# A hybrid SSD and attention block: x projection's weights in pairs of feature tiles, eight token buffers, scaling on two engines in turn

## Chip, core and metric

The kernel runs on one core of one Trainium2 chip. The metric is the device time of one execution in microseconds (us); runs of the kernel before and of the changed one are compared by their medians.

## The reference, cut to what matters

```
def hybrid_layer(x, ...):                      # x: (1, 1024 tokens, 1024), float32
    h = rmsnorm(x, norm_mix_w)
    proj = h @ w_in                            # (1024 x 5664)
    z, xbc, dt_raw, q, k, v = jnp.split(proj, offs, axis=-1)
    y_ssm = ssd_mixer(z, xbc, dt_raw, ...)     # conv over time and SiLU on xbc, then chunked SSD
    y_na = neighbourhood_attention(q, k, v, ...)
    x = x + jnp.concatenate([y_ssm, y_na], axis=-1) @ w_out
    h = rmsnorm(x, norm_mlp_w)
    return x + jnp.square(jax.nn.relu(h @ w_mlp_in)) @ w_mlp_out
```

The change touches the beginning: the norm of x, its transpose, and the columns of `w_in` for `xbc` (1536 columns, twelve feature tiles of 128), called the x projection here.

## The kernel before, in words

Every product is made of three matmuls: each operand is split into hi (rounded, by ScalarE) and lo (the rest, by VectorE or GpSimd), and `mm3` adds hi·hi, hi·lo and lo·hi.

**Tokens.** The 1024 tokens are eight tiles t of 128 (x0 to x7 below). For each, SP loads `xt` (512 KB), an engine multiplies it by the norm's weights into `hn`, TensorE transposes `hn` in two halves of four (`ptn`, in PSUM), ScalarE writes the hi part `hTh` of each half and VectorE the lo part `hTl`. ScalarE also writes the squares' sum over `xt` in place (`sumsq`), three tiles later in the code, from which GpSimd makes the norm's factor `rcol`; TensorE spreads it over partitions (`dg` by VectorE, then the matmul `prr`, then `rrow` by ScalarE), and it scales the projection behind the matmuls. `xt` has six buffers, `hn` two; tiles 2 and 5 are multiplied on GpSimd, the others on VectorE. The two halves of a tile take their PSUM buffers from two tags of two buffers each, so a half waits until `hTh` and `hTl` of the same half two tiles before are written; `pp`, the transpose of a few parameters (`prow`), takes its buffer from the second tag, behind the second half of tile 7.

**Weights.** `load_w` loads 1024 columns' worth into a raw buffer (three of them), ScalarE writes hi, `lo_eng` lo (four slots). For the x projection `load_w_col` takes one feature tile, all 1024 rows by 128 columns, 512 bytes a row. Two tiles are loaded early, among the tokens (`early`, at t of 3 and 5). Feature tiles 8 to 11 come first (the SSD's B and C), in two pairs, with GpSimd for lo; then dt (`decays`), then tiles 0 to 7 one at a time, with VectorE for lo.

**Order.** `xbc` computes, for each token half h and each of its feature tiles, 24 matmuls (`proj_col`: eight k of `mm3`) into a PSUM buffer `px`, scales it into `ub`, and convolves `ub` over time (`conv`). A list scheduler places the instructions of all engines, each engine's queue being strictly in the order it fixed. SP's queue holds all loads, in order; behind the beginning's loads it has eight small transfers of the position biases (`t1_dr`, `t_dr` in the profile), which a later stage needs. Behind the x projection come z, the SSD, attention, the output projection and the MLP, which the change does not touch.

Of the kernel before, what the change touches and what calls it, by code (L numbers as in the profile page):

```python
# [9 lines left out]
F32 = mybir.dt.float32  # L10
# [3 lines left out]
AF = mybir.ActivationFunctionType  # L14
# [4 lines left out]
P = 128  # L19
T = 1024  # L20
D = 1024
NT = T // P
KD = D // P
PROJ = 5664
OFF_Z, OFF_X, OFF_DT, OFF_Q, OFF_K, OFF_V = 0, 1024, 2560, 2592, 3616, 4640
# [30 lines left out]
def hymba_block(  # L56
# [25 lines left out]
    nc = tc.nc  # L82
# [48 lines left out]
    half = cp.tile([P, 8], F32, name="half")  # L131
    nc.gpsimd.memset(half, -0.5)

    def load_w(view, lo_eng, n=1024):
        pool = phase["w"][phase["n"] % len(phase["w"])]
        nb = phase["w"].count(pool)
        phase["n"] += 1
        rpool = phase["r"][phase["n"] % len(phase["r"])]
        raw = rpool.tile(
            [P, 1024], F32, tag="wraw", name="wraw", bufs=phase["r"].count(rpool)  # L140
        )
        hi = pool.tile([P, 1024], F32R, tag="wh", name="wh", bufs=nb)
        lo = pool.tile([P, 1024], F32R, tag="wl", name="wl", bufs=nb)
        dst = raw[:, 0:n]
        if len(view.shape) == 3:
            dst = dst.rearrange("p (a f) -> p a f", a=view.shape[1])
        nc.sync.dma_start(dst, view)
        nc.scalar.activation(hi[:, 0:n], raw[:, 0:n], AF.Copy)  # L148
        lo_eng.tensor_tensor(  # L149
            lo[:, 0:n], raw[:, 0:n], hi[:, 0:n].bitcast(F32), op=sub  # L150
        )
        return hi, lo
# [11 lines left out]

        return get

    def load_w_col(src, c0, n, lo_eng):
        v = src[:, c0 : c0 + n]
        hi, lo = load_w(v.rearrange("(k p) f -> p k f", p=P), lo_eng, KD * n)

        def get(k):
            s = slice(k * n, (k + 1) * n)
            return hi[:, s], lo[:, s]

        return get

    def mm3(pt, ah, al, bh, bl, first, last):
        nc.tensor.matmul(pt, lhsT=ah, rhs=bh, start=first, stop=False)  # L178
# [2 lines left out]

    def split_from_psum(hi, lo, src, scalar=None):
        if scalar is None:
            nc.scalar.activation(hi, src, AF.Copy)  # L184
            nc.vector.tensor_tensor(lo, src, hi.bitcast(F32), op=sub)
        else:
            nc.scalar.activation(hi, src, AF.Copy, scale=scalar)
            nc.vector.scalar_tensor_tensor(
                lo, src, scalar, hi.bitcast(F32), op0=mul, op1=sub
            )  # L190
# [14 lines left out]
    def transpose_split(th, tl, t, hn):  # L205
        for g in range(2):
            pt = (ps_tp if g else ps_s)("ptn")
            for j in range(4):
                k = 4 * g + j
                nc.tensor.transpose(  # L210
                    pt[:, j * P : (j + 1) * P], hn[:, k * P : (k + 1) * P], ident
                )
            dst = (slice(None), slice(4 * g, 4 * g + 4), slice(t * P, (t + 1) * P))
            split_from_psum(th[dst], tl[dst], pt.rearrange("p (j t) -> p j t", j=4))

# [1 line left out]
    with ExitStack() as ph:  # L219
        enter_phase(ph, 1, 3, 1)  # L220
        hp = ph.enter_context(tc.tile_pool(name="hp", bufs=1))
        hTh = hp.tile([P, KD, T], F32R, name="hTh")
        hTl = hp.tile([P, KD, T], F32R, name="hTl")
# [14 lines left out]
        with ExitStack() as p0:  # L238
            xp = p0.enter_context(tc.tile_pool(name="xp", bufs=2, side="right", reuse_waits="tile"))
            wb = xp.tile([P, D], F32, name="wb", bufs=1)  # L240
            ssq = xp.tile([P, NT], F32, name="ssq", bufs=1)
            xb = x[0].rearrange("(i b j) d -> i b j d", b=8, j=8)
            xts = []
            early = {}

            def sumsq(t):
                nc.scalar.activation(
                    xts[t], xts[t], AF.Square, accum_out=ssq[:, t : t + 1]
                )

            for t in range(NT):
                xt = xp.tile([P, D], F32, tag="xt", name="xt", bufs=6)
                xts.append(xt)
                hn = xp.tile([P, D], F32, tag="hn", name="hn", bufs=2)
                eng = nc.gpsimd if t in (2, 5) else nc.vector
                for h in range(2):
                    s = slice(h * 512, (h + 1) * 512)
                    if t == 0:
                        nc.sync.dma_start(
                            wb[:, s], norm_mix_w.partition_broadcast(P)[:, 0, s]  # L260
                        )
                        nc.sync.dma_start(xt[:, s], xb[:, t, :, s])
                        if h == 0:
                            nc.sync.dma_start(ident, cst_d[:, 0:P])
                        eng.tensor_tensor(hn[:, s], xt[:, s], wb[:, s], op=mul)
                if t > 0:
                    nc.sync.dma_start(xt, xb[:, t])
                    eng.tensor_tensor(hn, xt, wb, op=mul)
                transpose_split(hTh, hTl, t, hn)
                if t >= 3:  # L270
                    sumsq(t - 3)
                if t in (3, 5):
                    ft = 8 + (3, 5).index(t)
                    early[ft] = load_w_col(w_in[0], OFF_X + ft * P, P, nc.gpsimd)
            for t in range(NT - 3, NT):
                sumsq(t)
            for h in range(2):
                s = slice(4 * h, 4 * h + 4)
                nc.gpsimd.tensor_scalar(rcol[:, s], ssq[:, s], 1.0 / D, EPS, op0=mul, op1=add)
                nc.gpsimd.tensor_tensor(rcol[:, s], rcol[:, s], half[:, s], op=ALU.pow)  # L280
# [30 lines left out]
        with ExitStack() as p1:  # L311
# [114 lines left out]

            def xbc(fts):
                todo = []
                for ft in fts:
                    eng = nc.gpsimd if ft > 7 else nc.vector  # L430
                    get = early.get(ft) or load_w_col(w_in[0], OFF_X + ft * P, P, eng)
                    ub = qp.tile([P, T + 4], F32, tag="ub", name="ub")
                    nc.gpsimd.memset(ub[:, 0:2], 0.0)
                    nc.gpsimd.memset(ub[:, T + 2 : T + 4], 0.0)
                    todo.append((ft, get, ub))
                for h in range(2):
                    for ft, get, ub in todo:
                        pt = ps_mm("px")
                        proj_col(get, P, h, pt)
                        nc.vector.tensor_tensor(  # L440
                            to_grid(ub[:, 2 : T + 2], h),
                            from_blocks(pt),
                            from_blocks(rrow[:, h * 512 : (h + 1) * 512]),
                            op=mul,
                        )
                for ft, get, ub in todo:
                    conv(ft, ub)
# [43 lines left out]
            xbc((8, 9))  # L491
            xbc((10, 11))
            decays()
            for ft in range(8):
                xbc((ft,))


            szb = sz_dr.rearrange("c p f -> (c p) f").rearrange(
# [2 lines left out]
            for g in range(2):  # L501
                get = load_w_nat(w_in[0], 0, KD, OFF_Z + 512 * g, nc.vector)
                for t in range(NT):
                    pt = ps_mm("pz")
# [268 lines left out]
    with ExitStack() as ph:  # L773
# [63 lines left out]
        done = [0]  # L837
# [539 lines left out]
```

## Time and profile before

| | |
|---|---|
| time, median of 3 runs | 1728.23 us (1726.64 to 1728.27) |
| the profiled execution | 1725.33 us, its span 1723.5 us |
| TensorE busy | 1636.0 us, 95% of the span |
| VectorE, ScalarE, GpSimd busy | 1106.3, 726.5, 705.6 us (64, 42, 41%) |
| TensorE's granted clock, mean of the span | 0.98 of full |

The span is what the trace covers of the execution; 1.83 us lie around it. Times in the rows count from the span's start. In a timeline's row the first number is the start, the second the length, and in brackets stands how long the engine was idle before it and what ended that. PE is TensorE's matmul, PEld its weight load, DVE VectorE, ACT ScalarE, POOL GpSimd, SP or SPq the queue that issues the loads. A matmul of 512 columns is listed with 0.39 us, but the next starts 0.23 us behind it, since they overlap; the pitch is what counts.

### The profile page before, as it was taken

The numbers are of one execution on the slowest core, as the hardware profiler recorded it, in microseconds if no ns is written. First come the engines' busy times: TensorE is split into PE (matmuls) and PEld (weight loads), VectorE is DVE, ScalarE is ACT, GpSimd is POOL, SyncE is SP. The second block draws the span as 40 slices with busy tenths as digits, with TensorE's granted clock in tenths as the row PEclk, the third lists the DMA queues.
The fourth block names the chain that finished last, engine by engine and source line by source line (L and its number), as shares of the span: only waits on it lengthen the run. The fifth ranks groups of instructions, "written<-read, shape, count | busy, mean of one in ns | idle before, by whom it ended". The sixth has DMA issues, their size and how long they took to land. (4 is left out here: it accounts for less than half of the span.)

```text
span 1723.5 us, 20879 instructions
## 1 busy us (share of the span) xinstructions
PE 1636.0 (95%) x7461; PEld 1304.6 (76%) x7461; DVE 1106.3 (64%) x1687; ACT 726.5 (42%) x1189; POOL 705.6 (41%) x496
## 2 busy tenths in 40 slices
PE   6999999989888999999999988999999978999999
PEld 5788888777766777777767767788888866888887
DVE  5767214889787744778787776454343359787863
ACT  5434223434344434555565533454444443333330
POOL 4000004888778741221242242244444426555551
PEclk9999999999998999999999999999999989999999
DMA  8213338876675796754453141254344394644231
GB/s 200 62 37 104 89 98 242 210 195 207 213 206 161 234 311 199 240 150 138 132 183 123 56 159 49 73 190 153 134 159 147 125 349 149 201 141 166 92 110 73
DMA packets 178499, 269.75 MB, mean 157 GB/s; under 512 B 13963, under 2 KB 105051, under 8 KB 178395
## 3 DMA queue, kind: packets, MB, share of 16 engines
q1 hardware_dynamic: 135419, 231.18, 42.6%
q10 hardware_dynamic: 42976, 37.23, 7.1%
q8 instruction: 59, 0.97, 0.2%
q14 instruction: 45, 0.37, 0.1%
HBM read 185.21 MB, written 86.50 MB: 158 GB/s over the span
## 5 line engine op out<-in xcount | busy, mean ns | idle before, releaser
L760 POOL TENSOR_TENSOR wl<-wraw,wh 128x1024 fp32r<-128x1024 f32 x110 | 300.1, 2740 | 350.1 <-ACT wh L759 336.7
L745 PE MATMUL px<-wh,ahl 128*128 128x512 f32 x512 | 163.7, 397 | 9.8 <-ACT ahl L759 9.8
L759 ACT ACTIVATE wh<-wraw 128x1024 fp32r<-128x1024 f32 x110 | 115.7, 1054 | 127.4 <-issue 42.4
L179 PE MATMUL pq<-wl,hTh 128*128 128x512 f32 x384 | 153.1, 400 | 4.6 <-DVE wl L149 4.4
L745 PE MATMUL px<-h,wh 128*128 128x512 f32 x496 | 156.5, 396 | 0.0
L178 PE MATMUL pq<-wh,hTh 128*128 128x512 f32 x384 | 153.1, 401 | 1.9 <-ACT wh L148 1.2
L180 PE MATMUL pq<-wh,hTl 128*128 128x512 f32 x384 | 151.9, 396 | 0.0
L759 ACT ACTIVATE ahl<-ar 128x1024 fp32r<-128x1024 f32 x56 | 58.9, 1053 | 173.0 <-PE px L745 89.6
L760 DVE TENSOR_TENSOR ahl<-ar,ahl 128x1024 fp32r<-128x1024 f32 x56 | 107.3, 1917 | 37.4 <-ACT ahl L759 36.2
L745 PEld LDWEIGHTS px<-wh,ahl 128*128 128x128 f32 x512 | 97.3, 190 | 31.9 <-ACT ahl L759 10.2
L745 PEld LDWEIGHTS px<-h,wh 128*128 128x128 f32 x496 | 93.4, 189 | 22.4
L149 DVE TENSOR_TENSOR wl<-wraw,wh 128x1024 fp32r<-128x1024 f32 x40 | 55.0, 1376 | 83.3 <-ACT wh L148 82.7
L878 POOL TENSOR_TENSOR mb<-braw,nam 128x256 f32<-128x256 f32 (+1 forms) x48 | 41.0, 884 | 159.7 <-DVE nmx L936 123.4
L184 ACT ACTIVATE pth<-ptp 128x384 fp32r<-128x384 f32 (+1 forms) x128 | 58.4, 459 | 107.8 <-PE ptp L959 106.8
L745 PE MATMUL px<-wl,ahl 128*128 128x512 f32 x256 | 100.9, 394 | 0.0
L745 PE MATMUL px<-h,wl 128*128 128x512 f32 x248 | 98.1, 396 | 0.0
L179 PEld LDWEIGHTS pq<-wl,hTh 128*128 128x128 f32 x384 | 73.2, 191 | 22.1 <-DVE wl L149 7.9
L149 POOL TENSOR_TENSOR wl<-wraw,wh 128x1024 fp32r<-128x1024 f32 x18 | 43.8, 2446 | 110.5 <-ACT wh L148 84.3
L745 PE MATMUL pz<-wh,ahl 128*128 128x512 f32 x256 | 82.8, 400 | 6.5 <-DVE acc L1330 5.0
L178 PEld LDWEIGHTS pq<-wh,hTh 128*128 128x128 f32 x384 | 72.9, 190 | 18.2 <-ACT wh L148 2.5
L180 PEld LDWEIGHTS pq<-wh,hTl 128*128 128x128 f32 x384 | 73.2, 191 | 14.7
L612 POOL TENSOR_TENSOR rb<-rb,c 128x512 f32<-128x512 f32 x64 | 75.0, 1192 | 21.5 <-DMA rb<-cum_dr 18.7
(265 smaller groups left out, 4242.6 us busy)
## 6 DMA issues: line engine op xcount, KB each, us to landing
act_dr<-cq SPq DMA_DIRECT2D x56, 512.0 KB, 3.0
ar<-act_dr SPq DMA_DIRECT2D x56, 512.0 KB, 3.8
wraw<-in_w_in_dram SPq DMA_DIRECT2D x44, 512.0 KB, 4.0
rb<-cum_dr SPq DMA_DIRECT2D x32, 512.0 KB, 7.6
wraw<-in_w_mlp_in_dram SPq DMA_DIRECT2D x32, 512.0 KB, 4.7
wraw<-in_w_mlp_out_dram SPq DMA_DIRECT2D x32, 512.0 KB, 5.3
q_dr<-hl ACTq DMA_DIRECT2D x64, 128.0 KB, 3.2
k_dr<-hl ACTq DMA_DIRECT2D x16, 512.0 KB, 3.2
```

Of the source, the lines that this page charges most:

```text
L149: lo_eng.tensor_tensor(lo[:, 0:n], raw[:, 0:n], hi[:, 0:n].bitcast(F32), op=sub)
L178: nc.tensor.matmul(pt, lhsT=ah, rhs=bh, start=first, stop=False)
L179: nc.tensor.matmul(pt, lhsT=ah, rhs=bl, start=False, stop=False)
L180: return nc.tensor.matmul(pt, lhsT=al, rhs=bh, start=False, stop=last)
L184: nc.scalar.activation(hi, src, AF.Copy)
L612: nc.gpsimd.tensor_tensor(rb[:, d], rb[:, d], c1[:, d, c, h0 : h0 + 4].unsqueeze(2).broadcast_to([P, 4, P]), op=sub,)
L745: nc.tensor.matmul(pt, lhsT=a, rhs=b, start=f, stop=l, skip_group_check=True)
L759: nc.scalar.activation(hl[0], src, AF.Copy)
L760: eng.tensor_tensor(hl[1], src, hl[0].bitcast(F32), op=sub)
L878: nc.gpsimd.tensor_tensor(mb[:, s].rearrange("p (s r c) -> p s r c", r=16, c=8), v[:, a:b], nam[:, s].rearrange("p (s r c) -> p s r c", r= ...
```

## The change

The x projection's weights are loaded for two feature tiles at once: `load_w_pair` makes two tiles of 512 rows by 256 columns (1 KB a row), each with the columns of both features, and gives a getter for either feature. The first pair (8, 9) is loaded at t = 3, the second (10, 11) at t = 5; the two tiles of the first are called W0 and W1 below, those of the second W2 and W3 (in the kernel before, these are the tiles of features 8 to 11). All twelve feature tiles now run in pairs. For the early pairs, hi is placed behind the last hi part of the token tile just transposed (`issue_after`, which sets the order only). `xt` has eight buffers, and the odd token tiles are multiplied on GpSimd, the even ones on VectorE.

```
--- before.py
+++ after.py
@@ -131,7 +131,7 @@
     half = cp.tile([P, 8], F32, name="half")
     nc.gpsimd.memset(half, -0.5)
 
-    def load_w(view, lo_eng, n=1024):
+    def load_w(view, lo_eng, n=1024, after=None):
         pool = phase["w"][phase["n"] % len(phase["w"])]
         nb = phase["w"].count(pool)
         phase["n"] += 1
@@ -145,7 +145,8 @@
         if len(view.shape) == 3:
             dst = dst.rearrange("p (a f) -> p a f", a=view.shape[1])
         nc.sync.dma_start(dst, view)
-        nc.scalar.activation(hi[:, 0:n], raw[:, 0:n], AF.Copy)
+        with tc.issue_after(after.ins) if after else ExitStack():
+            nc.scalar.activation(hi[:, 0:n], raw[:, 0:n], AF.Copy)
         lo_eng.tensor_tensor(
             lo[:, 0:n], raw[:, 0:n], hi[:, 0:n].bitcast(F32), op=sub
         )
@@ -164,15 +165,21 @@
 
         return get
 
-    def load_w_col(src, c0, n, lo_eng):
-        v = src[:, c0 : c0 + n]
-        hi, lo = load_w(v.rearrange("(k p) f -> p k f", p=P), lo_eng, KD * n)
-
-        def get(k):
-            s = slice(k * n, (k + 1) * n)
-            return hi[:, s], lo[:, s]
-
-        return get
+    def load_w_pair(src, c0, lo_eng, after=None):
+        tiles = []
+        for kh in range(2):
+            v = src[512 * kh : 512 * (kh + 1), c0 : c0 + 2 * P]
+            tiles.append(load_w(v.rearrange("(k p) f -> p k f", p=P), lo_eng, after=after))
+
+        def half(j):
+            def get(k):
+                hi, lo = tiles[k // 4]
+                s = slice((k % 4) * 2 * P + j * P, (k % 4) * 2 * P + j * P + P)
+                return hi[:, s], lo[:, s]
+
+            return get
+
+        return half(0), half(1)
 
     def mm3(pt, ah, al, bh, bl, first, last):
         nc.tensor.matmul(pt, lhsT=ah, rhs=bh, start=first, stop=False)
@@ -181,8 +188,9 @@
 
     def split_from_psum(hi, lo, src, scalar=None):
         if scalar is None:
-            nc.scalar.activation(hi, src, AF.Copy)
+            done = nc.scalar.activation(hi, src, AF.Copy)
             nc.vector.tensor_tensor(lo, src, hi.bitcast(F32), op=sub)
+            return done
         else:
             nc.scalar.activation(hi, src, AF.Copy, scale=scalar)
             nc.vector.scalar_tensor_tensor(
@@ -211,7 +219,8 @@
                     pt[:, j * P : (j + 1) * P], hn[:, k * P : (k + 1) * P], ident
                 )
             dst = (slice(None), slice(4 * g, 4 * g + 4), slice(t * P, (t + 1) * P))
-            split_from_psum(th[dst], tl[dst], pt.rearrange("p (j t) -> p j t", j=4))
+            done = split_from_psum(th[dst], tl[dst], pt.rearrange("p (j t) -> p j t", j=4))
+        return done
 
 
 
@@ -249,10 +258,10 @@
                 )
 
             for t in range(NT):
-                xt = xp.tile([P, D], F32, tag="xt", name="xt", bufs=6)
+                xt = xp.tile([P, D], F32, tag="xt", name="xt", bufs=8)
                 xts.append(xt)
                 hn = xp.tile([P, D], F32, tag="hn", name="hn", bufs=2)
-                eng = nc.gpsimd if t in (2, 5) else nc.vector
+                eng = nc.gpsimd if t % 2 else nc.vector
                 for h in range(2):
                     s = slice(h * 512, (h + 1) * 512)
                     if t == 0:
@@ -266,12 +275,12 @@
                 if t > 0:
                     nc.sync.dma_start(xt, xb[:, t])
                     eng.tensor_tensor(hn, xt, wb, op=mul)
-                transpose_split(hTh, hTl, t, hn)
+                turned = transpose_split(hTh, hTl, t, hn)
+                if t in (3, 5):
+                    ft = 8 + (t - 3)
+                    early[ft] = load_w_pair(w_in[0], OFF_X + ft * P, nc.gpsimd, turned)
                 if t >= 3:
                     sumsq(t - 3)
-                if t in (3, 5):
-                    ft = 8 + (3, 5).index(t)
-                    early[ft] = load_w_col(w_in[0], OFF_X + ft * P, P, nc.gpsimd)
             for t in range(NT - 3, NT):
                 sumsq(t)
             for h in range(2):
@@ -426,9 +435,10 @@
 
             def xbc(fts):
                 todo = []
-                for ft in fts:
-                    eng = nc.gpsimd if ft > 7 else nc.vector
-                    get = early.get(ft) or load_w_col(w_in[0], OFF_X + ft * P, P, eng)
+                ft = fts[0]
+                eng = nc.gpsimd if ft > 7 else nc.vector
+                gets = early.get(ft) or load_w_pair(w_in[0], OFF_X + ft * P, eng)
+                for ft, get in zip(fts, gets):
                     ub = qp.tile([P, T + 4], F32, tag="ub", name="ub")
                     nc.gpsimd.memset(ub[:, 0:2], 0.0)
                     nc.gpsimd.memset(ub[:, T + 2 : T + 4], 0.0)
@@ -491,8 +501,8 @@
             xbc((8, 9))
             xbc((10, 11))
             decays()
-            for ft in range(8):
-                xbc((ft,))
+            for ft in range(0, 8, 2):
+                xbc((ft, ft + 1))
 
 
             szb = sz_dr.rearrange("c p f -> (c p) f").rearrange(
```

The scheduler's order moves with it. On SP W0 and W1 now stand in front of x4 and W2 in front of x6; before, the tile of feature 8 stood in front of x4 and that of feature 9 in front of x6. On TensorE four matmuls of the projection now stand in front of tile 5's transposes and those of the first half of tile 6; before, 24 stood in front of tile 5's.

In SP's queue, behind the token loads, these rows stand before (wraw_469 and 478 are the tiles of features 10 and 11):

```order
L298 DMA cst_297<-cst_dram 128x384
L301 DMA lmask_299<-lmask_dram 128x128
L303 DMA dsk_301<-in_d_skip_dram 128x16
L147 DMA wraw_469<-in_w_in_dram 128x8x128
L147 DMA wraw_478<-in_w_in_dram 128x8x128
L527 DMA t1_dr_76<-in_rel_pos_bias_dram 16x15x24 x8
L147 DMA wraw_714<-in_w_in_dram 128x8x128
```

and now (wraw_243 is W3):

```order
L307 DMA cst_309<-cst_dram 128x384
L310 DMA lmask_311<-lmask_dram 128x128
L312 DMA dsk_313<-in_d_skip_dram 128x16
L537 DMA t1_dr_76<-in_rel_pos_bias_dram 16x15x24 x8
L147 DMA wraw_243<-in_w_in_dram 128x4x256
L147 DMA wraw_714<-in_w_in_dram 128x4x256
```

W3 has moved behind the eight transfers of the position biases; its raw buffer is the one that held W0.

On ScalarE, at the end of the token stage, these rows stand before (ptn_217 and 224 are the halves of tile 5, 242 and 249 of tile 6, 261 and 268 of tile 7; wh_470 and 479 are hi of features 10 and 11):

```order
L247 ACTIVATE xt_238,ssq_109<-xt_238 128x1024
L148 ACTIVATE wh_470<-wraw_469 128x1024
L184 ACTIVATE hTh_89<-ptn_217 128x4x128
L148 ACTIVATE wh_479<-wraw_478 128x1024
L184 ACTIVATE hTh_89<-ptn_224 128x4x128
L184 ACTIVATE hTh_89<-ptn_242 128x4x128
L247 ACTIVATE xt_257,ssq_109<-xt_257 128x1024
L184 ACTIVATE hTh_89<-ptn_249 128x4x128
L184 ACTIVATE hTh_89<-ptn_261 128x4x128
L184 ACTIVATE hTh_89<-ptn_268 128x4x128
```

and now (ptn_223 and 230 are the halves of tile 5, 254 and 261 of tile 6, 273 and 280 of tile 7; wh_238 and 244 are hi of W2 and W3):

```order
L191 ACTIVATE hTh_89<-ptn_223 128x4x128
L256 ACTIVATE xt_250,ssq_109<-xt_250 128x1024
L191 ACTIVATE hTh_89<-ptn_230 128x4x128
L149 ACTIVATE wh_238<-wraw_237 128x1024
L191 ACTIVATE hTh_89<-ptn_254 128x4x128
L149 ACTIVATE wh_244<-wraw_243 128x1024
L256 ACTIVATE xt_269,ssq_109<-xt_269 128x1024
L191 ACTIVATE hTh_89<-ptn_261 128x4x128
L191 ACTIVATE hTh_89<-ptn_273 128x4x128
L191 ACTIVATE hTh_89<-ptn_280 128x4x128
```

Hi of W3 stands in front of hTh of the second half of tile 6 and of both halves of tile 7.

On GpSimd, through the token stage, these rows stand before (hn_152 and 214 are tiles 2 and 5):

```order
L268 TENSOR_TENSOR hn_152<-xt_151,wb_108 128x1024
L149 TENSOR_TENSOR wl_190<-wraw_188,wh_189 128x1024
L279 TENSOR_SCALAR rcol_104<-ssq_109 128x4
L268 TENSOR_TENSOR hn_214<-xt_213,wb_108 128x1024
L280 TENSOR_TENSOR rcol_104<-rcol_104,half_78 128x4
L149 TENSOR_TENSOR wl_234<-wraw_232,wh_233 128x1024
L149 TENSOR_TENSOR wl_471<-wraw_469,wh_470 128x1024
L149 TENSOR_TENSOR wl_480<-wraw_478,wh_479 128x1024
```

and now (hn_134, 170, 220, 270 are tiles 1, 3, 5, 7; wl_189 and 195 are lo of W0 and W1):

```order
L277 TENSOR_TENSOR hn_134<-xt_133,wb_108 128x1024
L277 TENSOR_TENSOR hn_170<-xt_169,wb_108 128x1024
L288 TENSOR_SCALAR rcol_104<-ssq_109 128x4
L289 TENSOR_TENSOR rcol_104<-rcol_104,half_78 128x4
L277 TENSOR_TENSOR hn_220<-xt_219,wb_108 128x1024
L150 TENSOR_TENSOR wl_189<-wraw_187,wh_188 128x1024
L150 TENSOR_TENSOR wl_195<-wraw_193,wh_194 128x1024
L277 TENSOR_TENSOR hn_270<-xt_269,wb_108 128x1024
L150 TENSOR_TENSOR wl_239<-wraw_237,wh_238 128x1024
L150 TENSOR_TENSOR wl_245<-wraw_243,wh_244 128x1024
```

Lo of W0 has moved from before tile 5's multiplication to behind it.

## Rows read from the trace of the kernel before

**Rows 1.** Busy time by stretches of 5 us: engines, granted clock, DMA share, GB/s

```profile
15.00:20.00 5.00, 3.67 (x16) 3.27 (x16) 1.91 (x3) 2.66 (x5) 0.97 (x2) 1.00 1.06 232
20.00:25.00 5.00, 0.98 (x5) 1.01 (x6) 4.44 (x5) 3.90 (x8) 4.84 (x3) 0.83 1.10 245
25.00:30.00 5.00, 5.00 (x15) 3.97 (x15) 3.56 (x3) 3.12 (x5) 4.12 (x3) 0.50 0.37 100
```

**Rows 2.** Waits of TensorE, 30 to 285 us, whole answer: total, times, longest

```profile
PE px L178 <- ACT hTh L184: 0.2, 1, 0.2
```

**Rows 3.** Timeline 0 to 30 us: what started as loads landed, and SP

```profile
15.76 1.23 DVE L268 TENSOR_TENSOR hn<-xt,wb 128x1024 f32<-128x1024 f32 x1 [0.67 <-DMA xt<-in_x_dram]
...
18.71 1.06 ACT L148 ACTIVATE wh<-wraw 128x1024 fp32r<-128x1024 f32 x1 [1.72 <-DMA wraw<-in_w_in_dram]
...
20.56 2.71 DVE L268 TENSOR_TENSOR hn<-xt,wb 128x1024 f32<-128x1024 f32 x1 [2.98 <-DMA xt<-in_x_dram]
...
22.73 0.22 SPq L288 DMA_DIRECT2D prow<-in_k_norm_w_dram  x1
...
25.68 0.22 SPq L287 DMA_DIRECT2D prow<-in_q_norm_w_dram  x1
...
27.00 0.22 SPq L288 DMA_DIRECT2D prow<-in_k_norm_w_dram  x1
...
27.27 0.37 SPq L298 DMA_DIRECT2D cst<-cst_dram  x1
...
28.35 0.33 SPq L303 DMA_DIRECT2D dsk<-in_d_skip_dram  x1
28.72 1.06 SPq L147 DMA_DIRECT2D wraw<-in_w_in_dram  x2
```

**Rows 4.** The same timeline: GpSimd, VectorE and TensorE

```profile
19.84 2.35 POOL L149 TENSOR_TENSOR wl<-wraw,wh 128x1024 fp32r<-128x1024 f32 x1 [4.03 <-ACT wh L148]
...
24.02 1.09 PE L210 MATMUL ptn<-ident,hn 128*128 128x128 f32 x4 [4.48 <-DVE hTl L185]
...
26.82 2.38 POOL L149 TENSOR_TENSOR wl<-wraw,wh 128x1024 fp32r<-128x1024 f32 x1
...
27.11 3.17 DVE L268 TENSOR_TENSOR hn<-xt,wb 128x1024 f32<-128x1024 f32 x1 [1.44 <-DMA xt<-in_x_dram]
...
27.46 0.63 PE L179 MATMUL px<-hTl,wh 128*128 128x512 f32 x1
...
27.89 0.63 PE L180 MATMUL px<-hTh,wl 128*128 128x512 f32 x1
```

**Rows 5.** Timeline 30 to 60 us

```profile
29.82 7.32 SPq L527 DMA_DIRECT2D t_dr<-in_rel_pos_bias_dram  x8
...
33.24 1.03 PE L210 MATMUL ptn<-ident,hn 128*128 128x128 f32 x8
33.32 1.06 ACT L148 ACTIVATE wh<-wraw 128x1024 fp32r<-128x1024 f32 x1 [1.81 <-DMA wraw<-in_w_in_dram]
...
37.09 1.06 ACT L247 ACTIVATE xt<-xt 128x1024 f32<-128x1024 f32 x1
...
38.13 0.60 ACT L184 ACTIVATE hTh<-ptn 128x512 fp32r<-128x512 f32 x1
...
38.76 0.69 DVE L185 TENSOR_TENSOR hTl<-ptn,hTh 128x512 fp32r<-128x512 f32 x1 [0.72 <-ACT hTh L184]
...
40.02 0.39 PE L179 MATMUL px<-hTl,wh 128*128 128x512 f32 x1
...
40.24 0.39 PE L180 MATMUL px<-hTh,wl 128*128 128x512 f32 x1
...
42.55 0.80 PE L179 MATMUL px<-hTl,wh 128*128 128x512 f32 x1
```

**Rows 6.** Timeline of SP, 32.0 to 32.6 us

```profile
31.59 1.26 SPq L527 DMA_DIRECT2D t_dr<-in_rel_pos_bias_dram  x2
```

**Rows 7.** Waits of SP's queue, 0 to 60 us: total, times, longest

```profile
SPq L267 <- ACT hTh L184: 3.7, 1, 3.7
```

## Prediction, made before the changed kernel was run

> **What bounds the kernel now.** I read the page's totals first, then busy time by stretches, then the waits of TensorE, and last the first 48 us instruction by instruction. The totals (the table above) make TensorE by far the busiest engine. The stretches say where the missing part is: from 15 to 25 us TensorE has a few microseconds of work while the DMA engines are full, and from 25 us on it is always busy [rows 1]. From 30 to 285 us, which takes in the whole x projection, it waited 0.2 us in all [rows 2]. So the x projection is bound by TensorE; what another engine saves there is worth nothing, and the change can act only through the moment at which TensorE gets its work in the first 48 us. Everything later follows as a block.
>
> What bounds that beginning are the loads. Between the landing of x3 (VectorE starts on it at 15.76) and that of x7 (SP, which waited for it, goes on at 28.35) lie six transfers of 512 KB: W0, x4, x5, W1, x6, x7 at 18.71, 20.56, 22.73, 25.68, 27.00, 28.35 [rows 3]. That is 2.1 us each, with full DMA engines until 25 us [rows 1].
>
> **The change, part by part.**
>
> *Same work.* A pair of tiles holds the same 1024 x 256 weights as two column tiles did: as many bytes, hi and lo operations, matmuls and transposes. That is 0. In the middle of the projection each pair now needs both its tiles to its end, so a slot comes free later; the next pair's tiles are already in the other two slots, and a pair is 96 matmuls of 0.227 us, 21.8 us, far above the 1.06 + 1.23 us of a split (the ScalarE row at 33.32 in [rows 5], and 1.23 for 1024 columns on VectorE at 15.76 in [rows 3]). I count 0 here, and a us or two if one splits late.
>
> *Eight token buffers.* x6 and x7 no longer wait for ScalarE to have finished with x0 and x1. The DMA engines are full anyway [rows 1], so this alone moves no landing: 0.
>
> *More weights ahead of the tokens.* The first pair puts W0 and W1 before x4, the second pair's first tile W2 before x6. In slots after x3, with the times of before for slots 3 and 6: x4 is third (22.7), x5 fourth (24.7, between 15.76 + 4 x 2.1 = 24.2 and the 25.7 of W1's slot), x6 sixth (28.4), x7 seventh (28.4 + 2.1 = 30.5). So x5 lands 2.0 later than now, x6 1.4 and x7 2.1.
>
> *GpSimd scales the odd tokens.* One costs 2.35 there (as the 1024-column operation at 19.84 in [rows 4]) against 1.23 on VectorE [rows 3]. More important is what happens when the two engines meet. VectorE's scaling at 20.56 took 2.71 and the one at 27.11 took 3.17; in both cases a GpSimd operation was running (19.84 + 2.35 = 22.19, 26.82 + 2.38 = 29.20), and VectorE's end is 1.08 behind the end of that operation [rows 3, 4]. So an SBUF-only operation of one waits out that of the other. The Trainium skill, GPSIMD Engine Reference, section Key points, says that GpSimd shares its SBUF interfaces with VectorE instructions of two SBUF inputs, which speaks against alternating them. By that rule, which gives no price, the sum would only be some unknown amount above 0; the trace agrees and gives the price, waiting to the end.
>
> *Chain A, over GpSimd.* x5 lands 24.7; scaling on GpSimd until 27.05; GpSimd's lo of W0, now behind it in order, 2.38, until 29.45; VectorE's scaling of x6 (landed 28.4) waits for that, until 30.7; VectorE's lo of the first half of token tile 4 stands behind it (0.69), until 31.4. Only then is the PSUM buffer free for the first half of tile 6, and TensorE's queue holds it ahead of all but four matmuls of the projection. Before, 24 of them were done when tile 5 began at 33.24 [rows 5]. From 31.4: half a tile (0.5), 41 matmuls at 0.227 (40.02 to 40.24 in [rows 5]), 12 transposes at 0.129 (1.03 for 8 at 33.24) = 0.5 + 9.3 + 1.55, so TensorE stands at the transpose of the parameters (pp) at 42.75. With what follows (pp 0.2, three matmuls 0.7, one 0.23, prr 0.43) the second matmul of the second token half would come at 44.3. It began at 42.55 before [rows 5]. Chain A alone costs 1.75.
>
> *Chain B, over SP and ScalarE.* The second pair's second tile, W3, needs a raw buffer that GpSimd frees at 29.45, and SP has it behind the eight t1_dr transfers, where W2 and W3 stood in front of them. x7 lands 30.5; cst, lmask and dsk take 1.2 (27.27 to 28.72, less some 0.2 of waiting, [rows 3]); eight t1_dr issues (t_dr in the profile) go at 0.65 each where nothing blocks them (31.59 to 31.59 + 1.26 is two, [rows 6]), 5.2; so W3 is issued at 36.9 and lands 4.6 later, as W2 did (28.72 to ScalarE's start at 33.32, [rows 3, 5]): 41.5. In ScalarE's order W3's hi stands in front of the squares of tile 7, of hTh of tile 6's second half and of both halves of tile 7. So: hi 1.06, squares 1.06, hTh 0.60, lo on VectorE 0.69 [rows 5], and the PSUM buffer that pp needs is free at 44.9, 2.2 after TensorE came for it. On the second token half: hTh of tile 7 at 44.8, then VectorE's dg, which waits out GpSimd's lo of W3 (42.6 + 2.4 = 45.0) and takes 0.69, then lo 0.69: 46.4. TensorE's second matmul there starts at 46.6 instead of 42.55: **+4.05 us**. Behind it I find nothing that it could overtake: from 48 us on the queues hold the same work, and TensorE has no waits to give up [rows 2].
>
> The profiled execution took 1725.33, 2.9 below the median of the runs shown, 1728.23; by its own time the sum is 1729.4, and set on the median 1728.23 + 4.05 = **1732.3**.
>
> *Bounds.* Low: if W2 cost the loads nothing (x7 at 28.35 as now), chain B ends 2.1 earlier and chain A's +1.75 decides. High: t1_dr issues at their old average (7.32 for eight, [rows 5]) add 2.1: +6.15. I take 0.65 because the two slow ones stood behind W2 and W3 in flight, and none flies now. The clock: TensorE worked at half pace (0.43 a matmul at 27.46 to 27.89, [rows 4]) from 24.02 until 30, the end of the stretch with granted 0.50 [rows 1]. Now it works from about 23.9 to 29.6 and then waits 1.8. If the rise comes only after that wait, up to 6 us more run at half pace, 3.0 lost on chain A, of which chain B hides 2.2: +4.85.
>
> **Rivals.** The threshold of all chances is 0.2%, 3.5 us: about what a measurement of this kernel can tell from no change.
>
> 1. *Chain B decides* (forecast): 1732.3, own range +2.5 to +6.2. For it: ScalarE's order and SP's order are fixed, and 5.2 + 4.6 us lie between x7 and W3. Against: the 2.2 us margin over chain A hangs on a few waits. 50%, of which about 10 in 50 end under 3.5.
>
> 2. *Chain A decides alone*, W3 in time: +1.75, 1730.0. It needs W3 at 39.3 or earlier. A W's landing came 2.95 behind its predecessor, an x's 1.85 and 2.17 [rows 3]; if the larger pieces (1 KB, not 512 B) took away these 0.9 us three times, x7 would land at 27.8 and W3 at 38.8. The Trainium skill, DMA: Bandwidth & Descriptors, section Specifications, asks 512 B or more for line rate: by that rule the larger pieces gain nothing and the sum stays at +4.05, and the rows, where an x is sometimes as late, do not settle it. With 0.9 us less for each W the sum falls to chain A's, itself 1 us or so earlier, near +0.5. 30%.
>
> 3. *The clock falls in the new wait* before pp (2.2 us and the waits of 1 us behind it): the 4.48 us of idling before 24.02 [rows 4] went with a granted clock that fell to 0.83, then 0.50 [rows 1], the lower of its two levels (1.2 of 2.4 GHz). It would cost up to 6 us at half pace, 3.0: +7, 1735.3. Against: the wait is half as long. 10%.
>
> 4. *Faster:* the loads of x6 and x7 were held by their issue. SP waited 3.7 us for ScalarE with x6 [rows 7]; if issued at once, x6 and x7 landed so much earlier, the squares, rrow and the second token half would follow, and TensorE's idle 4.48 us and the half pace shrink: 1728.23 - 3.7 = 1724.5. It decides if x7 lands before 24.6. Against: full DMA engines from 15 to 25 [rows 1], and one W more in front. 7%; 3% are left for no change at all.
>
> **How the numbers follow.** Slower by over 0.2%: 40 of rival 1's 50, rival 3's 10 and 5 of rival 2 with late tiles: 0.55. Faster: 0.07. Within 0.2%: the rest, 0.38. The range 1728.0 to 1736.5 reaches from rival 2's low end to rival 3's and leaves out the faster case and the worst sums.
>
> **What the profile after would show.** If right: the DMA waits put x7 at 30 or later; ScalarE waits for the DMA of W3 around 41 with hTh behind it; TensorE waits for lo of VectorE at pp for about 2 us; VectorE's scaling of x6 takes over 1.23 if it starts before GpSimd's lo ends; four matmuls of the projection, then tile 5 and a gap near 30; and from 48 us on the same rows come 4 us later. Wrong would be: no wait at pp (chain B falls), matmuls back to back from 27 us (chain A falls), or a second half-pace stretch behind 43 us (rival 3).

## The result, and the profile after

The changed kernel took 1732.06 us, the median of 12 runs (1722.24 to 1735.29), against 1726.31 for the kernel before in 12 runs (1720.39 to 1728.89): ratio 1.0030, 95% interval 1.0017 to 1.0043. That is slower, with an interval clear of 1; the ratio is above the 0.2% that a measurement of this kernel can tell from no change, though the interval's lower end is not. Two further sets of runs gave 1.0039 (1.0025 to 1.0052) and 1.0027 (1.0015 to 1.0040).

The execution that was profiled happens to be the shortest of its twelve (span 1720.4 us), so two later profiles of the same kernel, with spans of 1734.2 and 1726.7, stand beside it below. The stretches of the first, which answer to [rows 1] (engines, granted clock, DMA share, GB/s):

```profile
15.00:20.00 5.00, 2.70 (x12) 1.90 (x10) 3.55 (x6) 4.49 (x8) 2.74 (x3) 1.00 1.06 268
20.00:25.00 5.00, 4.43 (x20) 3.74 (x20) 1.67 (x3) 4.71 (x9) 4.20 (x2) 1.00 1.04 279
25.00:30.00 5.00, 2.68 (x9) 2.33 (x10) 4.26 (x6) 3.07 (x5) 5.00 (x3) 0.68 0.34 71
```

The DMA engines are as full as before but move 268 and 279 GB/s instead of 232 and 245, and TensorE's busy time goes the other way round: 4.43 us from 20 to 25, where it had 0.98, and then a hole from 25 to 30, where it had none. TensorE's waits from 30 to 285 us are again a single row, as in [rows 2], now at `pp`:

```profile
PE pp L299 <- DVE hTl L192: 0.8, 1, 0.8
```

The hole is chain A of the prediction. The timeline (start, length, engine) with what answers to [rows 3, 4]:

```profile
20.80 2.36 POOL L277 TENSOR_TENSOR hn<-xt,wb 128x1024 f32<-128x1024 f32 x1 [1.70 <-DMA xt<-in_x_dram]
...
23.12 5.68 POOL L150 TENSOR_TENSOR wl<-wraw,wh 128x1024 fp32r<-128x1024 f32 x2
...
24.47 2.10 DVE L277 TENSOR_TENSOR hn<-xt,wb 128x1024 f32<-128x1024 f32 x1 [3.33 <-DMA xt<-in_x_dram]
...
26.49 2.47 DVE L192 TENSOR_TENSOR hTl<-ptn,hTh 128x512 fp32r<-128x512 f32 x4
...
27.32 1.08 PE L218 MATMUL ptn<-ident,hn 128*128 128x128 f32 x4 [2.80 <-DVE hTl L192]
...
29.05 0.63 PE L186 MATMUL px<-hTl,wh 128*128 128x512 f32 x1
29.48 0.63 PE L187 MATMUL px<-hTh,wl 128*128 128x512 f32 x1
```

x5 is scaled on GpSimd, lo of W0 follows in its queue, VectorE's scaling of x6 (2.10 instead of 1.23) waits that out, lo of tile 4 stands behind it, and TensorE idles 2.80 us for the PSUM buffer. Behind it the granted clock is 0.68 in the stretch from 25 to 30, and the matmuls follow each other at 0.43 us until 30. Chain B comes after it, in the rows that answer to [rows 5, 6]:

```profile
26.16 0.36 SPq L307 DMA_DIRECT2D cst<-cst_dram  x1
...
32.76 8.61 SPq L147 DMA_DIRECT2D wraw<-in_w_in_dram  x4
...
37.46 1.06 ACT L149 ACTIVATE wh<-wraw 128x1024 fp32r<-128x1024 f32 x1 [7.79 <-DMA wraw<-in_w_in_dram]
...
38.42 1.04 ACT L256 ACTIVATE xt<-xt 128x1024 f32<-128x1024 f32 x1
...
39.46 1.55 ACT L191 ACTIVATE hTh<-ptn 128x512 fp32r<-128x512 f32 x3
40.07 0.69 DVE L192 TENSOR_TENSOR hTl<-ptn,hTh 128x512 fp32r<-128x512 f32 x1 [9.68 <-ACT hTh L191]
...
40.82 0.29 PE L299 MATMUL pp<-ident,prow 82*128 82x82 f32 x1 [0.81 <-DVE hTl L192]
```

x7 has landed when SP gets on to `cst` (26.16); the eight t1_dr issues stand between it and W3's load (32.76); ScalarE idles 7.79 us for W3, and squares, three hTh and lo follow before `pp`. The second profile of the changed kernel has the same rows some 2 us later:

```profile
22.32 2.38 POOL L277 TENSOR_TENSOR hn<-xt,wb 128x1024 f32<-128x1024 f32 x1 [2.54 <-DMA xt<-in_x_dram]
...
26.32 1.78 DVE L277 TENSOR_TENSOR hn<-xt,wb 128x1024 f32<-128x1024 f32 x1 [3.83 <-DMA xt<-in_x_dram]
...
28.17 0.37 SPq L307 DMA_DIRECT2D cst<-cst_dram  x1
...
28.85 1.09 PE L218 MATMUL ptn<-ident,hn 128*128 128x128 f32 x4 [2.76 <-DVE hTl L192]
...
39.72 1.06 ACT L149 ACTIVATE wh<-wraw 128x1024 fp32r<-128x1024 f32 x1 [8.52 <-DMA wraw<-in_w_in_dram]
...
43.08 0.29 PE L299 MATMUL pp<-ident,prow 82*128 82x82 f32 x1 [1.37 <-DVE hTl L192]
```

and the third has chain A's wait, and `pp` without one:

```profile
26.83 1.86 DVE L277 TENSOR_TENSOR hn<-xt,wb 128x1024 f32<-128x1024 f32 x1 [3.85 <-PE ptn L218]
27.86 0.36 SPq L307 DMA_DIRECT2D cst<-cst_dram  x1
...
29.44 0.97 PE L218 MATMUL ptn<-ident,hn 128*128 128x128 f32 x4 [2.62 <-DVE hTl L192]
...
38.73 1.06 ACT L149 ACTIVATE wh<-wraw 128x1024 fp32r<-128x1024 f32 x1 [6.94 <-DMA wraw<-in_w_in_dram]
...
42.21 0.23 PE L299 MATMUL pp<-ident,prow 82*128 82x82 f32 x1
```

So chain A's wait is in all three profiles, and chain B's in two of them. What they are worth, one profile cannot say. From 45 us on TensorE runs the x projection without a wait in every kernel but e6 (0.4 us), so the start of the first matmul of z that follows it (`pz`) sums up the beginning. It stood at 179.9, 182.2 and 181.3 us in the three profiles, and in the one of before at 179.9. The experiments had to show whether that one was typical, and which link costs.

### The profile page after: what moved, and what is told of

It reads as the page before. It is cut to its first block, busy times and chain, and to the rows that moved or that the text cites. A ratio compares the mean times of both kernels' runs of the same rounds, so it can differ in the third digit from the quotient of the medians.

```text
span 1720.4 us, 20867 instructions
## 1 busy us (share of the span) xinstructions
PE 1633.0 (95%) x7461; PEld 1302.8 (76%) x7461; DVE 1101.0 (64%) x1685; ACT 727.3 (42%) x1189; POOL 708.1 (41%) x498
## 3 DMA queue, kind: packets, MB, share of 16 engines
q1 hardware_dynamic: 129275, 231.18, 42.2%
```

## Experiments

All ratios are to the kernel before on the same chip, with their 95% intervals. The table has every run, with the start of the first z matmul in its profile, and there TensorE's wait for hTl before tile 6 (chain A) and at `pp` (chain B), in us.

| kernel | median us | ratio | first z | A | B |
|---|---|---|---|---|---|
| changed (first result) | 1732.1 | 1.0030 (1.0017 to 1.0043) | 179.9 | 2.8 | 0.8 |
| changed, a0_same | 1733.6 | 1.0039 (1.0025 to 1.0052) | 182.2 | 2.8 | 1.4 |
| changed, f4_changed_again | 1729.1 | 1.0027 (1.0015 to 1.0040) | 181.3 | 2.6 | 0 |
| A cut: e1_old_engines | 1734.4 | 1.0047 (1.0029 to 1.0065) | 184.6 | 0 | 3.8 |
| B cut: e4_hi_late | 1731.1 | 1.0026 (1.0013 to 1.0040) | 182.0 | 2.2 | 0 |
| both cut: f1_both_links_cut | 1726.3 | 1.0006 (0.9990 to 1.0022) | 177.8 | 0 | 0 |
| both cut: e3_second_pair_late | 1726.8 | 1.0004 (0.9991 to 1.0017) | 177.0 | 0 | 0 |
| the same, f3_late_again | 1724.0 | 0.9992 (0.9980 to 1.0005) | 178.1 | 0 | 0 |
| both cut: e5_late_old_engines | 1728.5 | 1.0008 (0.9995 to 1.0021) | 177.9 | 0 | 0 |
| both cut: f2_lo_on_vector | 1725.4 | 1.0000 (0.9982 to 1.0017) | 176.3 | 0 | 0 |
| e2_no_pairs | 1728.3 | 1.0019 (1.0008 to 1.0031) | 177.7 | | 0 |
| e6_eight_buffers | 1725.3 | 0.9996 (0.9983 to 1.0010) | 181.0 | | 0.8 |
| before, b0_before_again | 1726.1 | 0.9995 (0.9983 to 1.0006) | 177.5 | | 0 |

(The last three load single feature tiles. They too wait for hTl, 3.7 to 4.4 us, until 22 to 24.4 us, as [rows 4] show for before: another place. Two of the texts below give 182.0 and 177.6 for what stands here as 182.2 and 177.5. Several of the expected medians were missed by 0.3 to 3 us: e1 lies above its range, e2 just above, f1, f3 and f4 below theirs, a0's first z 0.8 below. Before's own median was 1725.0 beside the f runs and 1726.0 and 1726.5 beside the others, so the ratios are what is compared.)

**The two kernels once more, unedited.**

> The changed kernel once more, unedited. The profiled execution of it was 1722.2 us long, the shortest of twelve with a median of 1732.1, and in it the loads landed early (x7 at 26.2 us) and the first z matmul stood at 179.9 us as in the kernel before. Theory 'beginning': the typical execution is longer because chain B costs about 4 us in the first 47 us when loads land later; a profile of about 1732 us then has x7 at 28 us or later, the second matmul of the second token half at 45 to 47 us and the first z matmul at 183 to 185. Theory 'later': the beginning costs nothing in any execution; then the first z matmul stays at 180 +-0.7 in a profile of 1730 us or more, and the difference opens behind 285 us, where the clock falls in more places or where the order of instructions near 1050 us differs from the kernel before.

> The changed kernel a third time, beside the others on the same chip. Theory 'beginning': a median of 1732 to 1734 and a profile with the first z matmul at 180 to 184 us, which is 2 to 6 us behind before's second profile (177.6), with TensorE's waits for hTl of 2 to 3 us near 27 us and at pp of 0.8 to 4 us. If the profile has neither wait, the two links aren't what costs.

> The kernel before once more, unedited, for a second profile. The changed kernel's two profiles put the first z matmul at 179.9 and 182.0 us against 179.9 in the one profile of before; yet the median is 6 to 7 us longer, so some 4 us must be lost behind it, or that one profile of before began later than before does as a rule. Theory 'beginning': before's typical beginning is shorter than profiled, the first z matmul at 176 to 178 and no fall of the clock at 25 us. Theory 'later': the first z matmul at 179 to 181 again, and the stretch from 285 to 345 us shorter by 1.3 to 3.7 us than in the profiles of the variants, as in before's first profile.

The changed kernel came out slower both times, each time with chain A's wait; at `pp` TensorE waited 1.4 us in a0 and not at all in f4. The profile of the kernel before that the prediction was read from was a late one: the second has its first z matmul 2.4 us earlier, and no fall of the clock where [rows 1] had 0.83 and 0.50:

```profile
20.00:25.00 5.00, 2.94 (x11) 2.67 (x12) 3.71 (x5) 3.75 (x7) 4.84 (x5) 1.00 1.12 250
25.00:30.00 5.00, 5.00 (x19) 3.97 (x18) 4.11 (x3) 2.40 (x5) 2.19 (x1) 1.00 0.52 116
```

That speaks for the theory "beginning": the changed kernel's first z matmul is at 181.1 on the mean of three profiles, before's at 178.7 on that of two. One profile against another decides nothing here, since the beginning of one kernel moves by 2.4 us.

**Parts undone.** e1 gives the scaling back, e2 the pairs, e6 keeps the buffers alone:

```
e1:  eng = nc.gpsimd if t in (2, 5) else nc.vector      # in the changed kernel
e2:  xt ... bufs=8; eng = nc.gpsimd if t % 2 else nc.vector   # in the kernel before
e6:  xt ... bufs=8                                      # in the kernel before
```

> The changed kernel with the scaling given back as before: GpSimd for token tiles 2 and 5 only. Theory 'beginning': chain A goes (-1.75 at most), chain B stays, since W3's load stands behind the same eight transfers: 1730 to 1732 us. If chain A is what costs: 1726 to 1727. Theory 'later': the instructions near 1050 us stand as in the changed kernel, so 1731 to 1733, and the first z matmul at 180.

> The kernel before with eight buffers and the alternation, its single loads of 512 KB for one feature tile kept. Theory 'beginning' with chain B as the larger part: 1726 to 1728 us, no wait of ScalarE for W3 since each early load serves one feature tile; with chain A as the larger part: 1730 to 1732. Theory 'later': the order near 1050 us is that of the changed kernel here too, so 1731 to 1733.

> The kernel before with eight token buffers and nothing else: TensorE, VectorE, ScalarE and GpSimd keep their order, and only SP asks for the second early weight tile and the last token tiles sooner. The prediction holds it for nothing: 1726 +-1.5 us. If asking sooner helps: 1722 to 1724.

e6 is no change, as predicted. e1 did not win chain A's 1.75: it has no wait for hTl before tile 6, but chain B shows at its full length in its place, at `pp`:

```profile
40.34 1.06 ACT L149 ACTIVATE wh<-wraw 128x1024 fp32r<-128x1024 f32 x1 [6.50 <-DMA wraw<-in_w_in_dram]
...
43.26 0.29 PE L299 MATMUL pp<-ident,prow 82*128 82x82 f32 x1 [3.81 <-DVE hTl L192]
```

Behind that wait the granted clock is 0.73 from 45 to 50 us, which is rival 3 of the prediction as it was told, and e1's first z matmul is the latest of all:

```profile
45.00:50.00 5.00, 5.00 (x16) 3.30 (x15) 3.30 (x7) 0.81 (x2) 1.07 (x6) 0.73 0.36 103
```

e2 lies between: slower than before by 0.19%, though neither chain is in it and its first z matmul stands at 177.7. It differs from e6 by the alternation alone, and e6 is level with before. In its profile the time lies behind the first z matmul, 1552.5 us to the span's end against 1543.7 and 1546.6 in the two of before. What costs it there was not found; it stays open.

**The links cut.** In e3 the second pair is asked for after token tile 7, so that x6 and x7 go ahead of W2 (chain A's late x6 is gone) and the hi of W3 stand behind every hTh (chain B is gone). e4 leaves the loads up to W3 where the changed kernel has them and moves the hi and lo of W2 and W3 behind tile 7: chain B alone is cut. f1 is e4 with the scaling on the old engines: both links cut, the loads up to W3 in the same order. e5 is e3 with the old engines. The scheduler's order moves with the old engines: in e1 and f1 TensorE has 15 matmuls of the projection between the transposes of tile 5 and those of tile 6, where the changed kernel, e3 and e4 have none. So e1 and f1 cut chain A partly by that order.

```
e3:  -                if t in (3, 5):
     -                    ft = 8 + (t - 3)
     +                if t in (3, 7):
     +                    ft = 8 + (t - 3) // 2
e4:  (load_w keeps hi and lo of the second pair in `later`)
     +                if t == 7:
     +                    at.append(turned)         # issue_after the last hTh
     +                    for split in later:
     +                        split()
f1:  e4, and  eng = nc.gpsimd if t in (2, 5) else nc.vector
e5:  e3, and  eng = nc.gpsimd if t in (2, 5) else nc.vector
```

> The changed kernel with the second early pair (W2, W3) asked for after token tile 7 instead of 5: ScalarE's two hi of it stand behind all the hTh, so that the wait for W3's transfer holds nothing that the second token half needs, and x6 and x7 go ahead of W2 on SP. Theory 'beginning': chain B goes, pp's matmul comes 3 to 4 us earlier than in the unedited kernel's typical profile, 1727 to 1729 us. Theory 'later': 1731 to 1733, as the unedited kernel, since the order of instructions behind 285 us is the same.

> The kernel with the late second pair once more, unedited, beside the others on the same chip. Theory 'beginning': 1726 to 1728 again, the first z matmul at 177 +-1, level with the second profile of before (177.6). If the first run of it was lucky: 1729 or more.

> The changed kernel with all its loads where they are on SP (W3 still behind the eight t1_dr transfers), but ScalarE's hi of W2 and W3 and GpSimd's lo of them put behind the hTh of token tile 7. If ScalarE's place for the hi is the link by which chain B costs time: as the kernel with the second pair late, 1726 to 1728 us, pp's matmul near 38 us instead of 43. If the late load itself delays TensorE (the features 10 and 11 wait for W3): 1731 to 1734.

> The second pair asked for late (chain B gone) and the scaling on the old engines (GpSimd for tiles 2 and 5): the alternation alone, without chain B over it. If the alternation costs as chain A says (+1.75): 1725 us, 1.75 below the kernel with the late pair. If, as beside chain B (1734.4 against 1733.6), the alternation saves or costs nothing: 1727 to 1729.

> All loads in the changed kernel's order, W3 behind the eight t1_dr transfers and x6 behind W2; cut are only the two links on the engines: the scaling on the old engines (so that no lo of tile 4 waits behind VectorE's scaling of x6 while GpSimd works) and the hi of W2 and W3 behind the last hTh. With one link cut each, the medians were 1734.4 (scaling) and 1731.1 us (hi); with the order of loads changed, which cuts both, 1726.8 with the alternation and 1728.5 without. Theory 'two links that cover for each other': 1727 to 1729.5, no wait of TensorE for hTl and none at pp. Theory 'the later landing of x6 and W3 costs by itself': 1731 to 1734.

e4 missed its expectation, which named chain B alone. Its profile has no wait at `pp`, but chain A's with the slow matmuls behind it, and its first z matmul is as late as in the changed kernel (the timeline, and the stretch after it with a granted clock of 0.66; the clock had fallen once before, to 0.59 from 20 to 25, but so it had in f3, 0.54, which begins 3.9 us earlier):

```profile
30.18 0.63 PE L225 MATMUL ptn<-ident,hn 128*128 128x128 f32 x4 [2.18 <-DVE hTl L199]
...
42.72 0.23 PE L311 MATMUL pp<-ident,prow 82*128 82x82 f32 x1
```

```profile
30.00:35.00 5.00, 4.82 (x17) 3.91 (x18) 2.43 (x5) 2.55 (x5) 4.01 (x2) 0.66 0.38 76
```

In e3 VectorE's scaling of x6 gets in ahead of GpSimd's lo, TensorE waits 0.73 us in all behind 22 us, and `pp` is reached at 37.76:

```profile
21.39 2.38 POOL L277 TENSOR_TENSOR hn<-xt,wb 128x1024 f32<-128x1024 f32 x1 [1.72 <-DMA xt<-in_x_dram]
...
23.10 1.75 DVE L277 TENSOR_TENSOR hn<-xt,wb 128x1024 f32<-128x1024 f32 x1 [1.07 <-DMA xt<-in_x_dram]
...
23.72 5.73 POOL L150 TENSOR_TENSOR wl<-wraw,wh 128x1024 fp32r<-128x1024 f32 x2
...
27.14 0.50 PE L187 MATMUL px<-hTh,wl 128*128 128x512 f32 x1 [0.73 <-POOL wl L150]
...
37.76 0.23 PE L299 MATMUL pp<-ident,prow 82*128 82x82 f32 x1
```

f1 settles that it is the links and not the loads. In its profile x6, x7 and W3 come as late as in the changed kernel (27.03, 27.99 and 38.63), yet TensorE reaches `pp` at 38.08 without a wait, and its runs are level with before:

```profile
27.03 1.52 DVE L284 TENSOR_TENSOR hn<-xt,wb 128x1024 f32<-128x1024 f32 x1 [2.62 <-DMA xt<-in_x_dram]
...
27.99 0.36 SPq L319 DMA_DIRECT2D cst<-cst_dram  x1
...
31.05 0.60 PE L225 MATMUL ptn<-ident,hn 128*128 128x128 f32 x4
...
38.08 0.23 PE L311 MATMUL pp<-ident,prow 82*128 82x82 f32 x1
...
38.63 1.06 ACT L151 ACTIVATE wh<-wraw 128x1024 fp32r<-128x1024 f32 x1 [2.63 <-DMA wraw<-in_w_in_dram]
```

The five sets with a link left have a mean ratio of 1.0034 and a mean first z of 182.0; the five with both cut, 1.0002 and 177.4. So 0.32%, 5.5 us, go with 4.6 us in the beginning. From the first z matmul to the span's end the two groups do not differ: 1545.5 and 1545.9 us on the mean, and 1545.1 in the two profiles of before. That speaks against the theory "later", but single profiles lie between 1540.5 and 1552.5 there, so a loss of 2 us would not show. Nor does one profile's beginning tell what a kernel's runs do: e6 begins at 181.0 and is level with before. Cutting one link gives nothing back that the runs show, because the other one's delay was hidden behind it.

**A try at a faster kernel.** f2 is e3 with lo of W0 on VectorE:

```
+            lo = nc.vector if after and c0 == OFF_X + D and kh == 0 else lo_eng
```

> The kernel with the late second pair, and lo of its first early tile W0 on VectorE instead of GpSimd, so that TensorE's third matmul of a group doesn't wait for GpSimd (0.7 us there) and four matmuls go ahead of the transposes of token tile 5. If the beginning's last waits are worth something: the first z matmul 1 to 2 us earlier than in the late-pair kernel (about 177), 1724.5 to 1726 us. If TensorE is fed by the token loads anyway: 1726.8 +-1 as without it.

Its first z matmul is the earliest of all, 176.3, but that is 0.7 and 1.8 us ahead of e3 and f3, and the ratio is 1.0000. No version here is faster than the kernel before by more than 0.2%.

## Why the prediction was right, and where it was not

**The number** came out, 1732.3 against 1732.06, but so near by luck. The +4.05 was set on a median of 1728.23 from three runs, which is 1726.31 in twelve: 1.9 too high. Between the medians the change costs 5.75 us, by the three ratios 4.7 to 6.7: the cost was 1.7 too low, and the two cancel. Nor did TensorE come as late as the sum has it. The second matmul of the second token half was put at 46.6; in the three profiles of the changed kernel, and then in the second one of before, it starts here:

```profile
42.38 0.80 PE L186 MATMUL px<-hTl,wh 128*128 128x512 f32 x1
...
44.62 0.80 PE L186 MATMUL px<-hTl,wh 128*128 128x512 f32 x1
...
43.70 0.79 PE L186 MATMUL px<-hTl,wh 128*128 128x512 f32 x1
...
40.16 0.80 PE L179 MATMUL px<-hTl,wh 128*128 128x512 f32 x1
```

With the 42.55 of [rows 5] that is 43.6 against 41.4 on the mean, 2.2 us and not 4.05.

**Same work, and eight buffers:** 0 and 0, as said. In the changed kernel TensorE waits nowhere from 45 to 285 us, and e6 measures 0.9996.

**GpSimd scales the odd tokens:** the mechanism is as read from [rows 3, 4]: VectorE's end lies 1.08 behind the end of a GpSimd operation in e3 too (21.39 + 2.38 = 23.77 in GpSimd's row, 23.10 + 1.75 = 24.85). That agrees with the rule of the Trainium skill, GPSIMD Engine Reference, Key points, cited in the prediction. Its price depends on what stands beside it. With and without the alternation the ratios are 1.0039 and 1.0047 with chain B in place and 1.0004 and 1.0008 with the second pair late, so nothing; but 1.0026 and 1.0006 with chain B cut and the loads left (e4 and f1, chain A's price), and 1.0019 and 0.9996 with single loads (e2 and e6), where no wait was found for it.

**More weights ahead of the tokens** is the step that failed. x4, x5, x6 and x7 were put at 22.7, 24.7, 28.4 and 30.5. In the three profiles x4 came at 18.7, 20.1 and 20.6, x5 at 20.8, 22.3 and 22.9, x6 at 24.5, 26.3 and 26.8, x7 at 26.2, 28.2 and 27.9, no later than the 28.35 of before. The miss is there at x4 already; from x4 to x7 7.8 us were forecast and 7.5, 8.1 and 7.3 measured. Two things are in it, and how they share it was not measured. One is rival 2's larger pieces: from 5 to 25 us the changed kernel moved 280, 261 and 267 GB/s, the kernel before 246 and 244, and in the traces' packet records 512 B took 42 and 40 ns on the mean in the two profiles of before, 1 KB 61, 65 and 70 ns in the three of the changed kernel. The other is that the slots were read from a late profile: in the second one of before SP's queue puts x5, x6 and x7 at 20.9, 25.3 and 27.6, where [rows 3] have 22.7, 27.0 and 28.4. The Trainium skill, DMA: Bandwidth & Descriptors, Specifications, by which rows of 512 B already have line rate, does not agree with the packets' times; the measurement decides.

**Chain B** was right from x7's landing on. From x7 to ScalarE's start on W3 11.0 us were forecast; it was 11.3, 11.6 and 10.9. From there to `pp`, 3.4; it was 3.4 in the two profiles in which TensorE waited. Without chain A (e1) it makes TensorE wait 3.8. What was mis-sized is the margin over chain A: 2.2 forecast, 0.8 and 1.4 measured, and none in the third profile.

**Chain A** was right to the wait: from x5 to tile 6's transposes 6.7 forecast, 6.5 measured in all three profiles. It was then counted with full pace. From those transposes to the point where TensorE comes for `pp`, 11.35 were forecast and 12.7, 12.9 and 12.8 measured: the matmuls after the wait ran at half pace. That is 1.4 us by the fall of the clock. The prediction's bound on the clock had this case, with up to 3.0, but the sum did not; rival 3 had the fall at `pp`, where the changed kernel's three profiles do not show it and e1's does.

Together, chain B still decides in two of the three profiles, as in rival 1 but by 0.8 and 1.4 and not 2.2, and chain A alone in the third, as in rival 2. The 39.3 that rival 2 asked of W3 was for a TensorE that comes to `pp` at 42.75; it came at 40.0, 41.7 and 42.2, so W3 at 37.5 and 39.7 was late and at 38.7 in time. Rival 2's price, 1.75 at most, is not what the runs show (4.7 to 6.7). The direction and the place were right; the moments and the sizes were not.

**Open:** the profiles of the changed kernel put the beginning 2.4 us behind before's (181.1 against 178.7), while its runs are 4.7 to 6.7 us longer. Two and three profiles, each spread over 2.4 us, do not settle whether the beginning has it all. The sets with both links cut begin 1.3 us earlier than before and are not faster. A part may lie in the clock: the mean granted clock is 0.979 over the 48 runs with a link left and 0.981 over the 93 of before, 0.0023 of 1726 or up to 4 us. At the beginning the three profiles lose 1.7 us of it each, (1 - 0.68) x 5 + (1 - 0.98) x 5 in the first, but the two of before lose 3.4 and 0. Where the rest falls was not found.

## What to carry to other kernels

When two chains of waits end at nearly the same moment, undoing one shows nothing; cut both before judging either, and read in the profile which wait took the place of the one removed. What a late load costs depends on what stands behind its consumer in that engine's queue: here a hi part of weights that only the next pair of feature tiles needed stood in ScalarE's queue in front of the transposed tokens that TensorE needed now. And before a few microseconds are argued from one profile, take a second: the beginning of the same kernel moved by 2.4 us.

## What the runs showed of the hardware

- Rows of 1 KB moved faster than rows of 512 B in loads of 512 KB. From 5 to 25 us a packet of 512 B took 40 to 49 ns on the mean in the four profiles without pairs (10.5 to 12.8 bytes a ns), one of 1 KB 61 to 71 ns in the ten with them (14.4 to 16.7). With the token loads in it, the same stretch moved 226 to 249 GB/s (mean 241) and 249 to 280 (mean 264), at a DMA share of 1.02 to 1.06.
- TensorE ran at half pace while the profile's granted clock stood at 1.00. In e3 the stretches from 20 to 25 and from 25 to 30 us both have 1.00, yet the first matmuls follow each other at 0.43 us and the later ones at 0.23:

```profile
23.14 0.63 PE L186 MATMUL px<-hTl,wh 128*128 128x512 f32 x1
23.57 0.63 PE L185 MATMUL px<-hTh,wh 128*128 128x512 f32 x1
...
27.72 0.39 PE L186 MATMUL px<-hTl,wh 128*128 128x512 f32 x1
...
27.95 0.40 PE L187 MATMUL px<-hTh,wl 128*128 128x512 f32 x1
```

- Whether the clock falls after TensorE's idle stretch near 20 us differs between executions of one kernel: 0.83 and 0.50 in one profile of before, 1.00 and 1.00 in the other.
